# Block products for the last four up groups of an MLP, with the sums of weights made in DRAM

## The chip, the cores and the metric

The kernel runs on one core of a Trainium2 chip. Its metric is the device time of one execution in microseconds (us). The engines are TensorE (PE in the profile, with PEld for its loads of the stationary operand), VectorE (DVE), ScalarE (ACT), GpSimd (POOL) and SyncE (SP). They run at the same time, each works through its own list of instructions, and they wait for one another by semaphores. DMA transfers are issued here from SP, from ScalarE and from POOL.

## The reference

One layer of a hybrid encoder works on 512 rows of width 1024, all in float32. It has an input projection, eight heads of attention with a forget gate beside four heads of a gated recurrence, an output projection, cross attention to 256 memory rows, and an MLP. The change lies in the MLP:

```python
u = rmsnorm(h, norm_ff_g[l]) @ w1[l]
h = h + jnp.square(jax.nn.relu(u)) @ w2[l]
return rmsnorm(h, final_norm_g)
```

Here `w1` is 1024 x 4096 and `w2` is 4096 x 1024. The row factor of the inner norm is positive, so it can leave relu and square: the hidden value is r squared times relu(x w1) squared, with r one number per row.

## The kernel before

Every float32 operand of a matmul is split in two parts of a narrower format, `hi` and `lo`, and each product of a 128 x 128 stationary part with a moving part of up to 512 columns is made by three matmuls: hi hi, hi lo and lo hi. For a weight block, SP loads a raw tile, ScalarE casts it to `hi` (L175) and VectorE subtracts to get `lo` (L179). `whp` and `wlp` hold four blocks of each part, `wrp` two raw tiles.

The 4096 hidden columns are worked off in eight groups of 512. The up part of a group (`mlp_up`) makes four PSUM blocks of 128 hidden columns x 512 rows, each over eight chunks of depth 128 by `gemm_fm` (L240 to L242). ScalarE applies relu and square (L1306, L1307). The down part (`mlp_down`, L1366 to L1368) multiplies the 512 x 512 transposed hidden values with the 512 x 1024 rows of `w2`. It does so in 2 x 2 blocks with seven products in place of eight, named 1 to 7. Four of these products need sums of blocks of hidden values (`hidden_sums`, `hidden_part`), four need sums of blocks of `w2`. PSUM banks U, Y and V gather the products in the order of `PRODUCTS`, and after each product VectorE adds the bank, times plus or minus r squared (`rsq`), to the result `acc` (L1334). The down part of group g-1 follows the up part of group g. The last two groups share one down part, whose final product is cut in pieces with the final norm (`last_product`, L1393).

The sums of `w2` blocks are made in SBUF. `load_raws` loads five raw blocks per group (L1255) into a ring of eight slots. POOL issues DMAs that accumulate onto them (L1244): two add a block straight from `w2`, two add one slot to another once its former value has been split. For the up groups from the third on, four blocks of `w1` per group go through `load_unit`.

TensorE's order is the order in which the code emits it. The other engines are put in order by a planner, from priorities; the splits of the MLP have a lowered one (`ahead(PW)`). A queue of blocks, `unit_q`, keeps the next four blocks loaded and split ahead of the product in hand (`unit`).

Before the MLP, POOL computes the biases of attention (`bi`, L926, with rows of `nF` loaded by DMA), some row factors (L361, L364) and sums of squares (L1074 to L1078). Work of projections is mixed in between the steps of attention (`fill`).

Of the kernel before, what the change touches and what calls it, by code (L numbers as in the profile page):

```python
# [16 lines left out]
P = 128  # L17
# [21 lines left out]
NEG = -3.0e38  # L39


@with_exitstack
def emit(
# [189 lines left out]
    def gemm_fm(ps, wt, col, ahi, alo, n=S, order=range(KC), begun=False):  # L233
# [3 lines left out]
        for n_, k in enumerate(order):  # L237
# [5 lines left out]
            yield 3 * n / 2400  # L243

    def gemm_tm(ps, wt, ahi, alo, tb, nk=KC):
# [3 lines left out]
        for k in range(nk):  # L249
# [6 lines left out]
            yield 3 * n / 2400  # L256

    def gemm_wide(pss, ahi, alo, done):

        for half in range(2):  # L260
            whi, wlo = next_panel()
            for u in range(2):
                for tb, ps in enumerate(pss):
                    sl = slice(tb * P, (tb + 1) * P)
                    for kk in range(2):
# [5 lines left out]
                        yield 3 * S / 2400  # L271
# [127 lines left out]
    xTd = drp.tile([4, P, 2, S], F32, name="xTd")  # L399
    park = {}  # L400
# [817 lines left out]
    slots = [t[:, i, :] for t in [ap_.tile([P, 4, D], F32, tag="act", name=f"wq{j}") for j in range(2)] for i in range(4)]  # L1218
    HS = S // 2
    units, raws, unit_q = {}, {}, deque()  # L1220
    sqs, comb, hbs = {}, {}, {}

    def up_units(g):
        for j in range(2):
            spec = panel(w1, g * HG + j * WT)
            for n in range(2):

                def prep(g=g, j=j, n=n, spec=spec):
                    if (j, n) == (0, 0):
                        down_raws(g - 1)  # L1230
                    unit, splits = load_unit(f"u{g}{j}{n}", spec, slice(n * UK, (n + 1) * UK))
                    with ahead(PW):
                        for split in splits:
                            split()
                    units["u", g, j, n] = unit

                unit_q.append((("u", g, j, n), prep))

    quad = {"a1": (0, 0), "c1": (0, 0), "a2": (0, 1), "b2": (1, 1), "b1": (1, 0)}
    PRODUCTS = ("1", "2", "6", "5", "7", "3", "4")  # L1240

    def add_weights(raw, src):

        gp.dma_start(raw.rearrange("p (k n) -> p k n", k=2), src, accum_op=ALU.add)  # L1244
# [18 lines left out]
    def down_raws(g):  # L1263

        load_raws(g, RAWS)
        first_adds(g)
# [287 lines left out]
```

## Time and profile before

| | before |
|---|---|
| time, median of 3 runs | 766.79 us (766.42 to 766.93) |
| the profiled execution: time, span | 766.06 us, 764.3 us |
| TensorE busy, instructions | 755.3 us (99%), 4069 |
| VectorE busy | 502.8 us (66%) |
| ScalarE busy | 388.6 us (51%) |
| POOL busy | 170.3 us (22%) |
| granted TensorE clock | 0.999 |
| DMA | 103.01 MB, mean 135 GB/s |

The page of the profile tells for each engine the busy time, then cuts the span into 40 slices (19 us each) with the busy share in tenths. The chain of waits goes back from the last instruction to what released it, step by step, so an engine with a large share of the chain sets the time. A row of a group names the line, engine, operation, output and inputs, shapes and count, then the busy time, the mean duration in ns, and the idle time before these instructions with the engine that ended it. Records of matmuls overlap, so the rate of TensorE is read from start to start. A row of a stretch gives its bounds and, per engine, the busy time in it.

### The profile page before, as it was taken

How to read it: one execution, taken by the hardware profiler on the slowest of the kernel's cores; microseconds unless marked ns; L12 is line 12 of the kernel's file. 1: busy time of each engine (PE TensorE's matmuls, PEld its weight loads, DVE VectorE, ACT ScalarE, POOL GpSimd, SP SyncE). 2: the span in 40 equal slices, each digit the busy share in tenths (PEclk: the TensorE clock that was granted, in tenths of full speed). 3: DMA queues.
4: the chain of work that ended last, by engine and by line, in shares of the span. 5: the costliest groups of instructions: out<-in, count | busy, mean ns of one | idle time of the engine just before them, and what ended most of it. 6: DMA issues, size and time to landing. Idle time of an engine off the chain costs nothing.

```text
span 764.3 us, 10886 instructions
## 1 busy us (share of the span) xinstructions
PE 755.3 (99%) x4069; PEld 635.5 (83%) x4069; DVE 502.8 (66%) x816; ACT 388.6 (51%) x657; POOL 170.3 (22%) x248
## 2 busy tenths in 40 slices
PE   9999999999999999999999999999999999999996
PEld 6889888888889988888888888888888888888885
DVE  5647863678877656555546445939495776767596
ACT  6655554656666523344444456455454545353653
POOL 7207531322542225310000110101001010101123
PEclk9999999999999999999999999999999999999999
DMA  8652333313635432222113595575758575758602
GB/s 241 201 138 58 85 84 111 111 56 111 197 111 172 138 129 83 84 98 67 56 56 103 204 280 129 153 171 160 179 156 198 143 189 142 193 138 217 141 1 110
DMA packets 78870, 103.01 MB, mean 135 GB/s; under 512 B 4657, under 2 KB 56410, under 8 KB 78818
## 3 DMA queue, kind: packets, MB, share of 16 engines
q1 hardware_dynamic: 69266, 76.61, 32.1%
q0 software_dynamic: 8960, 24.67, 15.5%
q10 hardware_dynamic: 592, 1.05, 0.4%
q8 instruction: 32, 0.52, 0.3%
q14 instruction: 20, 0.16, 0.1%
HBM read 89.71 MB, written 4.21 MB: 123 GB/s over the span
## 4 chain that ended last, share of the span: by engine, by line
PE 95%; DVE 2%; ACT 1%; POOL 1%; issue 1%; ACTq 0%; POOLq 0%
PE u L240 8%; PE u L241 8%; PE u L242 8%; PE U L1366 4%; PE U L1367 4%; PE U L1368 4%; PE xq L240 2%; PE wo L240 2%; PE xq L241 2%; PE xq L242 2%; PE xw L241 2%; PE xw L242 2%; PE wo L242 2%; PE xw L240 2%; PE wo L241 2%; PE Y L1366 2%
## 5 line engine op out<-in xcount | busy, mean ns | idle before, releaser
L179 DVE TENSOR_TENSOR wld<-wq,whd 128x1024 fp32r<-128x1024 f32 x56 | 68.8, 1240 | 46.8 <-ACT whd L175 46.8
L240 PE MATMUL u<-x_hi,whu 128*128 128x512 f32 x192 | 74.7, 389 | 0.0
L241 PE MATMUL u<-x_lo,whu 128*128 128x512 f32 x192 | 74.7, 389 | 0.0
L242 PE MATMUL u<-x_hi,wlu 128*128 128x512 f32 x192 | 74.7, 389 | 0.0
L175 ACT ACTIVATE whd<-wq 128x1024 fp32r<-128x1024 f32 x56 | 58.3, 1052 | 29.7 <-PE u L241 18.5
L1244 POOL DMA_DIRECT2D wq<-in_w_dram x16 | 19.4, 1228 | 178.4 <-DMA wq<-in_w_dram 124.7
L175 ACT ACTIVATE whu<-wru 128x1024 fp32r<-128x1024 f32 x24 | 25.3, 1053 | 56.9 <-DMA wru<-in_w_dram 56.9
L179 DVE TENSOR_TENSOR wlu<-wru,whu 128x1024 fp32r<-128x1024 f32 x24 | 29.3, 1222 | 33.0 <-ACT whu L175 33.0
L1366 PE MATMUL U<-whd,hb 128*128 128x512 f32 x120 | 46.7, 389 | 0.0
L1367 PE MATMUL U<-wld,hb 128*128 128x512 f32 x120 | 46.7, 389 | 0.0
L1368 PE MATMUL U<-whd,hb 128*128 128x512 f32 x120 | 46.7, 389 | 0.0
L242 PEld LDWEIGHTS u<-x_hi,wlu 128*128 128x128 f32 x192 | 36.0, 188 | 7.5
L240 PEld LDWEIGHTS u<-x_hi,whu 128*128 128x128 f32 x192 | 36.0, 188 | 7.5
L241 PEld LDWEIGHTS u<-x_lo,whu 128*128 128x128 f32 x192 | 36.0, 188 | 7.4
L1244 POOL DMA_DIRECT2D wq<-wq x16 | 14.1, 880 | 125.0 <-DVE wld L179 95.6
L1334 DVE SCALAR_TENSOR_TENSOR acc<-U,rsq,acc 128x512 f32<-128x512 f32 x56 | 39.8, 744 | 0.3 <-PE U L1393 0.3
L926 POOL TENSOR_SCALAR bi<-nF,Ft 128x128 f32<-128x128 f32 (+3 forms) x32 | 23.0, 726 | 58.0 <-PE pt L958 37.0
L1306 ACT ACTIVATE sq<-u 128x512 f32<-128x512 f32 x32 | 18.7, 584 | 20.5 <-PE u L242 20.5
L1368 PEld LDWEIGHTS U<-whd,hb 128*128 128x128 f32 x120 | 22.5, 188 | 4.7
L1366 PEld LDWEIGHTS U<-whd,hb 128*128 128x128 f32 x120 | 22.5, 188 | 4.7
L1367 PEld LDWEIGHTS U<-wld,hb 128*128 128x128 f32 x120 | 22.5, 188 | 4.7
L1324 ACT ACTIVATE hb<-s 128x512 fp32r<-128x512 f32 x24 | 15.0, 629 | 20.6 <-PE U L1368 13.6
(957 smaller groups left out, 2262.1 us busy)
## 6 DMA issues: line engine op xcount, KB each, us to landing
wq<-in_w_dram SPq DMA_DIRECT2D x40, 512.0 KB, 3.4
wru<-in_w_dram SPq DMA_DIRECT2D x24, 512.0 KB, 6.4
wq<-in_w_dram POOLq DMA_DIRECT2D x16, 512.0 KB, 8.7
wq<-wq POOLq DMA_DIRECT2D x16, 512.0 KB, 4.9
xTd<-xT POOLq DMA_DIRECT2D x4, 512.0 KB, 4.1
nF<-Fd POOLq DMA_DIRECT2D x8, 256.0 KB, 3.9
hT<-xTd POOLq DMA_DIRECT2D x4, 512.0 KB, 5.3
xt<-in_x_dram SPq DMA_DIRECT2D x3, 512.0 KB
```

The source lines that it names most:

```text
L175: ac.activation(hi, raw, AF.Copy)
L179: ve.tensor_tensor(lo, raw, f(hi), ALU.subtract)
L240: te.matmul(ps, wh, hi, start=n_ == 0 and not begun, stop=False)
L241: te.matmul(ps, wh, lo, start=False, stop=False)
L242: te.matmul(ps, wl, hi, start=False, stop=k == order[-1])
L926: gp.tensor_scalar(bi[:, 0:n], fF[h][:, 0:n], -1.0, Ft[:, tb, h : h + 1], op0=ALU.mult, op1=ALU.add)
L1244: gp.dma_start(raw.rearrange("p (k n) -> p k n", k=2), src, accum_op=ALU.add)
L1306: ac.activation(u, ps, AF.Relu)
L1334: ve.scalar_tensor_tensor(a, ps, rsq[sign][:, tb : tb + 1], a, op0=ALU.mult, op1=ALU.add)
L1366: te.matmul(ps, hi, whi[:, k, :], start=begin, stop=False, skip_group_check=True)
L1367: te.matmul(ps, hi, wlo[:, k, :], start=False, stop=False, skip_group_check=True)
L1368: te.matmul(ps, lo, whi[:, k, :], start=False, stop=k == 1, skip_group_check=True)
```

## The change

The up parts of groups 4 to 7 (`SEVEN`) are also made in 2 x 2 blocks with seven products (`mlp_up7`): depth in two halves of 512, hidden columns in two halves of 256, rows in two halves of 256. Each product takes one block of four chunks, and its matmuls have 256 columns. The sums of blocks of x that four of the products need are made once, in groups 1 to 3 (`x_sums`). Banks pass their contents on by copies on ScalarE, and two blocks are completed by an add on VectorE before relu and square.

All sums of weight blocks, for `w2` in eight groups and for `w1` in four, are now made in DRAM (`sum_jobs`): each sum is a DMA that copies a block and a DMA that accumulates another onto it, eight transfers of 512 KB a set, twelve sets, all issued on POOL. `Presum` spreads their emission over the program: after 80 us of counted matmul time, one each 4.8, two sets in turn. Every product then has a block of its own to load, from the weights or from a sum, into one of five raw tiles (`raw_tile`: two from `wrp`, three from the pool `s4`). The ring of eight slots and the accumulations in SBUF go.

The order of the products becomes 1, 5, 6, 2, 7, 3, 4 in both parts. In the down part product 1 is copied from bank U to bank V by ScalarE, and product 2 adds to it, so the add of product 1 to `acc` goes. `acc` is multiplied once by the row's mean square (`e2`) so that r squared leaves the adds; the final norm takes this factor out again, with an epsilon to match (`eps3`). The hidden parts are made up to four ahead of use (`hidden_ahead`, `HB`).

```diff
+SEVEN = (4, 5, 6, 7)
+RAWS, HB = 5, 4
+PRE0, PRE = 80.0, 4.8
...
-            yield 3 * n / 2400
+            yield presum.tick(3 * n / 2400)
...
+
+    SUMS = {"5": ("00", "01"), "7": ("01", "11"), "6": ("5", "11"), "4": ("6", "10")}
+
+    def block1(g, rc):
+        r, c = int(rc[0]), int(rc[1])
+        n0 = g * HG + c * WT
+        return w1[r * S : (r + 1) * S, n0 : n0 + WT].rearrange("(k p) n -> p k n", p=P)
+
+    def block2(g, rc):
+        r, c = int(rc[0]), int(rc[1])
+        k0 = g * HG + r * 2 * P
+        return w2[k0 : k0 + 2 * P, c * S : (c + 1) * S].rearrange("(k p) n -> p k n", p=P)
+
+    wsum = {}
+
+    def sum_jobs(kind, g):
+        block, shape = (block1, [P, UK, WT]) if kind == "u" else (block2, [P, 2, S])
+        for name in SUMS:
+            wsum[kind, g, name] = drp.tile(shape, F32, name=f"ws{kind}{g}{name}")
+        for name, add in (("5", 0), ("7", 0), ("5", 1), ("7", 1), ("6", 0), ("6", 1), ("4", 0), ("4", 1)):
+            dst, (a, b) = wsum[kind, g, name], SUMS[name]
+            if add:
+                gp.dma_start(dst, block(g, b), accum_op=ALU.add)
+            else:
+                gp.dma_start(dst, wsum[kind, g, a] if a in SUMS else block(g, a))
+            yield
+
+    class Presum:
+        def __init__(self):
+            self.jobs, self.left = deque(), PRE0
+
+        def tick(self, us):
+            self.left -= us
+            while self.left <= 0.0 and self.jobs:
+                job = self.jobs[0]
+                if next(job, 0) == 0:
+                    self.jobs.popleft()
+                    continue
+                if len(self.jobs) > 1:
+                    self.jobs[0], self.jobs[1] = self.jobs[1], self.jobs[0]
+                self.left += PRE
+            return us
+
+    presum = Presum()
+    for g in range(DFF // HG):
+        presum.jobs.append(sum_jobs("d", g))
+        if g + 2 in SEVEN:
+            presum.jobs.append(sum_jobs("u", g + 2))
...
-    slots = [t[:, i, :] for t in [ap_.tile([P, 4, D], F32, tag="act", name=f"wq{j}") for j in range(2)] for i in range(4)]
...
-    units, raws, unit_q = {}, {}, deque()
+    units, unit_q = {}, deque()
     sqs, comb, hbs = {}, {}, {}
+    PRODUCTS = ("1", "5", "6", "2", "7", "3", "4")
+    QUAD = {"1": "00", "2": "10", "3": "11"}
+    raw_n = [0]
...
+    def raw_tile(name):
+        raw_n[0] += 1
+        if raw_n[0] % RAWS in (0, 2):
+            return wrp.tile([P, D], F32, tag="wr", name=f"wr{name}", padded_shape=[P, UK * UW])
+        return s4([D], f"wr{name}")
+
+    def add_unit(key, shape, src):
+
+        def prep():
+            name = "".join(map(str, key))
+            unit = new_parts(shape, name)
+            raw = raw_tile(name).rearrange("p (k n) -> p k n", k=shape[0])
+            nc.sync.dma_start(raw, src())
+            with ahead(PW):
+                split_of(unit[0], unit[1], raw)()
+            units[key] = unit
+
+        unit_q.append((key, prep))
...
+        if g in SEVEN:
+            for name in PRODUCTS:
+                add_unit(("u", g, name), [UK, WT], lambda name=name: block1(g, QUAD[name]) if name in QUAD else wsum["u", g, name])
+            return
...
-            spec = panel(w1, g * HG + j * WT)
...
-    def add_weights(raw, src):
-
-        gp.dma_start(raw.rearrange("p (k n) -> p k n", k=2), src, accum_op=ALU.add)
-
-    RAWS = ("a1", "c1", "a2", "b2", "b1")
-
-    def load_raws(g, names):
-        w = raws.setdefault(g, {})
-        for name in names:
-            r, c = quad[name]
-            n = 5 * g + RAWS.index(name)
-            w[name] = slots[n % 8] if n < 38 else k4([D], f"wq{n}")
-            src = w2[g * HG + r * 2 * P : g * HG + (r + 1) * 2 * P, c * S : (c + 1) * S].rearrange("(k p) n -> p k n", p=P)
-            nc.sync.dma_start(w[name].rearrange("p (k n) -> p k n", k=2), src)
-            w[name, "src"] = src
-
-    def first_adds(g):
-        w = raws[g]
-        add_weights(w["a2"], w["b2", "src"])
-        add_weights(w["c1"], w["a2", "src"])
...
-                for to, of in (("a1", "a2"), ("b1", "a1")):
-                    add_weights(w[to], w[of].rearrange("p (k n) -> p k n", k=2))
...
+                add_unit(("d", g, name), [2, S], lambda g=g, name=name: block2(g, QUAD[name]) if name in QUAD else wsum["d", g, name])
...
+    def mlp_up7(g):
+
+        qa, qb = (k4([2, S], f"sq{g}{j}") for j in range(2))
+        sqs[g, 0], sqs[g, 1] = qa, qb
+        h1, h2 = slice(0, HS), slice(HS, S)
+        bank = {}
+
+        for name in PRODUCTS:
+            b = {"5": "Y", "3": "Y", "2": "V"}.get(name, "U")
+            if b not in bank:
+                bank[b] = (pvt if b == "Y" else mm)(f"u{b}{g}").rearrange("p (i n) -> p i n", i=2)
+                if b == "V":
+                    pass
+            ps = bank[b]
+            whi, wlo = unit("u", g, name)
+            xh, xl = xsum[name]
+            for k in range(UK):
+                for i in range(2):
+                    ws, begin = slice(i * P, (i + 1) * P), name in "15" and k == 0 and i == 0
+                    te.matmul(ps[:, i, :], whi[:, k, ws], xh[:, k, :], start=begin, stop=False, skip_group_check=True)
+                    te.matmul(ps[:, i, :], whi[:, k, ws], xl[:, k, :], start=False, stop=False, skip_group_check=True)
+                    te.matmul(ps[:, i, :], wlo[:, k, ws], xh[:, k, :], start=False, stop=k == UK - 1, skip_group_check=True)
+                presum.tick(6 * HS / 2400)
+            if name == "1":
+                bank["V"] = mm(f"uV{g}").rearrange("p (i n) -> p i n", i=2)
+                ac.activation(bank["V"], ps, AF.Copy)
+            elif name == "5":
+                y5 = t2(f"y5{g}", F32, (2, HS))
+                ac.activation(y5, ps, AF.Copy)
+            elif name == "6":
+                ac.activation(bank["Y"], ps, AF.Copy)
+            elif name == "2":
+                square(ps, qa[:, :, h1])
+            elif name == "7":
+                ve.tensor_tensor(qb[:, :, h2], ps, y5, ALU.add)
+                square(qb[:, :, h2], qb[:, :, h2], -1.0)
+            elif name == "3":
+                ve.tensor_tensor(qb[:, :, h1], ps, y5, ALU.add)
+                square(qb[:, :, h1], qb[:, :, h1], -1.0)
+            else:
+                square(ps, qa[:, :, h2])
+            yield
...
+    def x_sums():
+
+        xs_hi, xs_lo = act_tile("xs_hi"), act_tile("xs_lo")
+        xs_hi, xs_lo = (t.rearrange("p k (h n) -> p (k h) n", h=2) for t in (xs_hi, xs_lo))
+
...
+        names = ("5", "6", "3", "7")
+        out_ = {n: tuple(t[:, i * UK : (i + 1) * UK, :] for t in (xs_hi, xs_lo)) for i, n in enumerate(names)}
+        d = s4([UK, HS], "xs_d")
+        for n, (a, b, sign) in (("5", ("4", "2a", -1)), ("6", (None, "1", 1)), ("3", (None, "2", -1)), ("7", ("1", "2a", -1))):
+            op = ALU.add if sign > 0 else ALU.subtract
+            if a is None:
+                ve.tensor_tensor(d, d, f(x_[b][0]), op)
+            else:
+                ve.tensor_tensor(d, f(x_[a][0]), f(x_[b][0]), op)
+                ve.tensor_tensor(d, d, f(x_[a][1]), ALU.add)
+            ve.tensor_tensor(d, d, f(x_[b][1]), op)
+            yield
+            hi, lo = out_[n]
+            ac.activation(hi, d, AF.Copy, scale=-1.0 if n == "6" else 1.0)
...
+                ve.tensor_tensor(lo, d, f(hi), ALU.subtract)
+            xsum[n] = (hi, lo)
+            yield
...
+    def hidden_ahead(key, n):
+
+        used = hb_order.index(key)
+        for k in hb_order[used : used + n]:
+            if k not in hbs and k[0] in comb:
+                hidden_part(*k)
...
-        ve.scalar_tensor_tensor(a, ps, rsq[sign][:, tb : tb + 1], a, op0=ALU.mult, op1=ALU.add)
...
+        a = acc[2 * rows + t][:, half * S : (half + 1) * S]
+        if sign > 0:
+            ve.tensor_tensor(a, ps, a, ALU.add)
+        else:
+            ve.scalar_tensor_tensor(a, ps, -1.0, a, op0=ALU.mult, op1=ALU.add)
...
-        "1": ("U", True, ((0, 0, 1),)),
+        "1": ("U", True, ()),
...
-        "2": ("V", True, ((0, 0, 1),)),
+        "2": ("V", False, ((0, 0, 1),)),
...
+                hidden_ahead((g, name), 1)
...
-                    banks[bank, t] = {"U": sc, "Y": tr, "V": mm}[bank](f"{bank}{g}{t}")
+                    banks[bank, t] = {"U": sc, "Y": tr}[bank](f"{bank}{g}{t}")
...
+                presum.tick(6 * S / 2400)
+                if g != gs[-1]:
+                    continue
+                if name == "1":
+                    banks["V", t] = mm(f"V{g}{t}")
+                    ac.activation(banks["V", t], ps, AF.Copy)
...
-            if not end:
-                hidden_part(gs[0] + 1, name)
-            elif n == 0:
-                hidden_part(NG - 1, PRODUCTS[1])
+            hidden_ahead((gs[-1], name), HB)
+            yield
...
-            gp.tensor_scalar(e, e, 1.0, EPS, op0=ALU.mult, op1=ALU.add)
+            gp.tensor_tensor(e, e, eps3[:, tb : tb + 1], op=ALU.add)
...
-                    for _ in range(2):
-                        unit_q.popleft()[1]()
-            else:
-                wt = tuple(list(x) for x in zip(*(unit("u", g, j, n) for n in range(2))))
-                if (g, j) == (NG - 1, 0):
-                    load_raws(g, RAWS[0:3])
...
+    xsum = {}
+
+    def mlp_up_group(g):
+        if g in SEVEN:
+            yield from mlp_up7(g)
+            return
...
-    rsqt = cp.tile([P, 2, NT], F32, name="rsq")
-    rsq = {1: rsqt[:, 0, :], -1: rsqt[:, 1, :]}
-    e2 = sm(NT, "r2e")
+    e2 = cp.tile([P, NT], F32, name="e2")
+    eps3 = cp.tile([P, NT], F32, name="eps3")
     gp.tensor_scalar(e2, ms2, 1.0, EPS, op0=ALU.mult, op1=ALU.add)
-    ve.reciprocal(rsq[1], e2)
...
+    gp.tensor_tensor(eps3, e2, e2, op=ALU.mult)
+    gp.tensor_scalar(eps3, eps3, EPS, 0.0, op0=ALU.mult, op1=ALU.add)
+    for tb in range(NT):
+        ac.activation(acc[tb], acc[tb], AF.Copy, scale=e2[:, tb : tb + 1])
...
+    sums = x_sums()
     for g in range(1, NG):
-        for up in mlp_up_group(g):
-            square(*up)
+        for n, _ in enumerate(mlp_up_group(g)):
+            hidden_ahead((g - 1, PRODUCTS[0]), min(n, HB))
+            if g < 4 and n == 1:
+                next(sums, None)
...
-            mlp_down((g - 1,))
-    load_raws(NG - 1, RAWS[3:])
-    first_adds(NG - 1)
-    hidden_part(NG - 1, PRODUCTS[0])
...
+            for n, _ in enumerate(mlp_down((g - 1,))):
+                if g < 4 and n in (2, 5):
+                    next(sums, None)
+
+    hidden_ahead((NG - 2, PRODUCTS[0]), HB)
```

More of the change, by code (lines that the diff above doesn't have):

```diff
@@ L1294, in unit, with square @@
         return got
+    def square(ps, out_, sign=1.0):
+        ac.activation(out_, ps, AF.Relu, scale=sign)
+        ac.activation(out_, out_, AF.Square)
     def mlp_up(g, j, wt):
@@ L1411, in last_product @@
                 product(ps, 1, qs, True)
-                ve.scalar_tensor_tensor(acc[3][:, qs], ps, rsq[1][:, 3:4], acc[3][:, qs], op0=ALU.mult, op1=ALU.add)
+                ve.tensor_tensor(acc[3][:, qs], ps, acc[3][:, qs], ALU.add)
                 v = squares(3, o3, qs, v, f"fv3{q}")
```

89 lines of the change are left out of this document (35 added, 54 removed).

## The prediction

> **What bounds the kernel now.** I read the page first (busy time, slices, chain), then the waits of TensorE, then stretches of the MLP stage, then groups and transfers.
>
> ```profile
> span 764.3 us, 10886 instructions
> ...
> PE 755.3 (99%) x4069; PEld 635.5 (83%) x4069; DVE 502.8 (66%) x816; ACT 388.6 (51%) x657; POOL 170.3 (22%) x248
> ...
> PE   9999999999999999999999999999999999999996
> ...
> DMA  8652333313635432222113595575758575758602
> ...
> q1 hardware_dynamic: 69266, 76.61, 32.1%
> q0 software_dynamic: 8960, 24.67, 15.5%
> ...
> PE 95%; DVE 2%; ACT 1%; POOL 1%; issue 1%; ACTq 0%; POOLq 0%
> ```
>
> TensorE is the bound from end to end: 99% busy, 95% of the chain. Its whole list of waits is two lines, and neither lies in the MLP:
>
> ```profile
> PE warm L352 <- DVE ones L356: 1.3, 1, 1.3
> PE pt L958 <- DVE bi L950: 0.7, 1, 0.7
> ```
>
> So only fewer or cheaper matmuls make it faster, and every wait that the change puts in front of TensorE is paid in full. Two stretches of the MLP, one early and one in its regular middle (columns: bounds, length, busy of PE, weight load, DVE, ACT, POOL, clock, DMA share, GB/s):
>
> ```profile
> 440.00:460.00 20.00, 20.00 (x90) 16.57 (x89) 9.56 (x13) 11.73 (x19) 2.60 (x3) 1.00 1.10 285
> ...
> 640.00:680.00 40.00, 40.00 (x179) 33.10 (x178) 28.00 (x36) 19.55 (x26) 4.18 (x4) 1.00 0.67 171
> ```
>
> TensorE is full in both, even where the DMA share is 1.10.
>
> **The change, part by part.** *Matmuls.* The price is the start-to-start time, not the duration (389 ns records overlap). The end of the chain gives it for both shapes, twelve with 512 columns and then twenty-four with 256:
>
> ```profile
> 751.77 2.72 PE U L1393 x12
> 754.49 2.88 PE Z L1393 x24
> ```
>
> 2.72/12 = 0.2267 us and 2.88/24 = 0.120 us. Half the columns cost 53% of the time, which eats part of the saving. An up group was 4 blocks x 8 chunks x 3 = 96 wide matmuls, 21.76 us. With seven block products it is 7 x 4 x 2 x 3 = 168 narrow ones, 20.16 us. Saved: 1.60 us a group, **6.4 us** in four groups. The down groups keep 84 wide matmuls, 19.04 us.
>
> The Trainium skill, "TensorE: Matmul & The Clock Gate", section "Back-to-back issue gap", gives a lone gap of N/2.4 + 2.5 ns, so 215.8 and 109.2 ns here; an estimate from it is 20.72 - 18.34 = 2.37 us a group and 9.5 us in all. The trace has 226.7 and 120, both about 11 ns above that, and more instructions pay the extra more often; the sum stays with 6.4.
>
> *VectorE and ScalarE beside TensorE.* Prices come from the groups in 520 to 720 us:
>
> ```profile
> L179 DVE TENSOR_TENSOR wld<-wq,whd 128x1024 fp32r<-128x1024 f32 x34 | 41.1, 1221 | 30.0 <-ACT whd L175 30.0
> L1334 DVE SCALAR_TENSOR_TENSOR acc<-U,rsq,acc 128x512 f32<-128x512 f32 x38 | 27.0, 744 | 0.0
> ...
> L1328 DVE TENSOR_TENSOR hb<-sq,hb 128x512 fp32r<-128x512 f32 x15 | 10.3, 686 | 1.1 <-ACT hb L1324 1.1
> ```
>
> ```profile
> L175 ACT ACTIVATE whd<-wq 128x1024 fp32r<-128x1024 f32 x34 | 35.2, 1050 | 14.4 <-PE u L241 12.7 <-DMA wq<-wq 1.7
> L175 ACT ACTIVATE whu<-wru 128x1024 fp32r<-128x1024 f32 x20 | 21.1, 1053 | 47.4 <-DMA wru<-in_w_dram 47.4
> L1307 ACT ACTIVATE sq<-sq 128x512 f32<-128x512 f32 x19 | 12.0, 633 | 0.6
> L1306 ACT ACTIVATE sq<-u 128x512 f32<-128x512 f32 x20 | 11.7, 583 | 9.7 <-PE u L242 9.7
> ```
>
> VectorE per round of one up and one down group, before: 11 splits x 1.22 + 14 adds x 0.744 + 11 halves and sums x 0.686 = 31.4 us of 40.8. After: 14 x 1.22 + 8 signed adds x 0.744 + (4 plain adds, 11 halves and sums, 2 adds in the up part) x 0.686 = 34.7 us of 39.2. ScalarE before: 11 x 1.05, 8 square steps of 0.583 or 0.633, 7 halves near 0.633, 20.9 us; after: three more splits and five bank copies at about 0.6, 27.0 us. Both stay under 39.2, so I cost them at nothing. The cover is lookahead (four blocks split ahead, four hidden halves) and, for the banks, one product between write and rewrite: 24 x 0.120 = 2.88 us in the up part, where U is copied by ScalarE after product 1 and again after 6, and read by VectorE after 7. A copy of 0.6 behind a split of 1.05 fits in 2.88. The sums of x (14 VectorE operations near 1.22, 17 us, plus four ScalarE casts) are spread over groups 1 to 3, some 6 us a round beside the 31.4, less two adds: 36 of 40.8, covered, with little left. Scaling acc once is four ScalarE passes near 1.05 us before the first add, and the rsq chain goes; nothing on TensorE. The tail keeps its instructions: nothing.
>
> *Loads on SP.* 64 become 92 transfers of 512 KB.
>
> ```profile
> wq<-in_w_dram SPq DMA_DIRECT2D x40, 512.0 KB, 3.4
> wru<-in_w_dram SPq DMA_DIRECT2D x24, 512.0 KB, 6.4
> wq<-in_w_dram POOLq DMA_DIRECT2D x16, 512.0 KB, 8.7
> wq<-wq POOLq DMA_DIRECT2D x16, 512.0 KB, 4.9
> ```
>
> A round needs 14 blocks where it needed 11 and 4 accumulations, one each 2.8 us. With five raw tiles that leaves 14 us from request to split, against landings of 3.4 to 6.4. A load of a sum waits on SP for its last accumulation, and the loads behind it wait too. By the pacing in the code (first job at 80 us of counted matmul time, one per 4.8, 96 in all) the last pair of sums is issued at 541 counted us; the MLP starts at about 326 (3 x columns/2400 summed over the matmul triples of the projections before it), a round counts 41 and one with block products 38, so the last down products start at 588 and their loads some 10 earlier; the closest pair has some 35 us to spare: nothing.
>
> *Copies and accumulations on POOL.* 32 accumulations leave, 96 transfers come, 51 of them before the MLP. Engine time of one: no transfer from DRAM to DRAM is in this trace. Two stretches with a lone accumulation, and one with a load:
>
> ```profile
> 554.00:556.00 2.00, 2.00 (x11) 1.65 (x9) 1.23 (x1) 0.34 (x2) 0.25 (x1) 1.00 0.67 131
> 556.00:558.00 2.00, 2.00 (x10) 1.69 (x9) 1.16 (x2) 1.92 (x3) 0.00 (x0) 1.00 0.71 131
> ...
> 560.00:562.00 2.00, 2.00 (x11) 1.65 (x10) 2.00 (x4) 0.93 (x3) 0.00 (x0) 1.00 1.03 385
> ```
>
> An accumulation takes 2 x (0.67 + 0.71) = 2.76 us of all 16 engines for its 0.524 MB, a load 0.524/0.385 x 1.03 = 1.40. I take 1.40 for a copy (nearest to a load: one stream) and 2.76 for an accumulation, bounds 1.40 and 2.76 for both: 48 x 4.16 = 200 us, between 134 and 265, spread over some 550 us of the run. In the MLP, loads take 0.67 x 40.8 - 4 x 2.76 = 16.3 us per 11, 1.48 each: 40% of the engines in groups 1 to 3, 53% in the last four. With paced sums (8.5 jobs per round, 2.08 each, 43%) that is 83 to 96%: tight, not over. I cost it at 0, because the row at 440 shows full engines and a full TensorE; its upper end is the first rival.
>
> POOL's own time is on the path at one place before the MLP:
>
> ```profile
> L1244 POOL DMA_DIRECT2D wq<-in_w_dram x16 | 19.4, 1228 | 178.4 <-DMA wq<-in_w_dram 124.7
> ```
>
> ```profile
> 150.11 1.03 POOL hr L364
> 151.16 0.44 POOL bi L926 x2
> ...
> 154.24 0.55 POOL m1r L364
> 154.81 1.10 DVE mt L374
> ...
> 163.87 0.30 PE pt L958
> ```
>
> The chain runs through POOL from 150 to 155 us and reaches the `pt` where TensorE waited its 0.7 us. An issue is 1.23 us; between zero and two fall into that stretch (one job per 4.8 counted us, about 6 real): 0 to 2.5 us. I take one, **+1.2**. Elsewhere `bi` waits for TensorE, not the reverse. An accumulation also waits at the head of POOL's queue for its copy to land, and `bi` and the loads of nF stand behind it; jobs of one set are two slots apart, about 12 us, over 8.7: nothing, and up to a few us if landing stretches.
>
> **Sum.** The profiled execution took 766.06 (span 764.3, the rest around it): 766.06 - 6.4 + 1.2 = 760.9. The median of the runs is 766.79, 0.7 above that execution, so 761.6. A measurement of this kernel can tell about 0.2%, 1.5 us, from no change.
>
> **Rivals.** *Loads starve (slower).* After r2e POOL has nothing but sums until the last adds, so nothing paces them:
>
> ```profile
> 441.59 0.18 POOL L1505 TENSOR_SCALAR r2e<-ms 128x4 f32<-128x4 f32 x1 [2.30 <-ACT sj L1501]
> ...
> 730.59 3.00 POOL L1458 TENSOR_TENSOR fa<-acc,gfin 128x512 f32<-128x512 f32 x2 [8.18 <-DVE acc L1334]
> ```
>
> 45 transfers, 94 us of engine time, would run in one block beside the loads. A packet of POOL's queue took 0.155 x 764.3 x 16/8960 = 211 ns, one of SP's 57 ns. If the queues take turns packet by packet, loads get 57/268 = 21%. The block then lasts 94/0.79 = 119 us, loads get 25 us of it where 40% of 119 = 48 are needed, and the nine blocks in hand (five raw, four split) are worth 9 x 1.48 = 13: TensorE advances 38/0.40 = 96 us in 119 and stands for 23. Time: 761.6 + 23 = 785. It decides from a share of about 28% for the loads downwards. Against it: each accumulation waits for a landing, so about two are in flight and the queue is often empty; 440 to 460. For it: a share of 96% without any burst.
> The Trainium skill, "DMA: Bandwidth & Descriptors", section "Queues, rings and completion order", says that each DMA engine goes round its queues packet by packet, which is this rule; the 6.4 us of the wru loads beside accumulations against 3.4 lean to it, but no wait of TensorE does.
>
> *A split holds the bank copies (slower).* ScalarE already stood 47.4 us for wru loads in that window, 2.4 per split of 20. If a split that waits so stands ahead of the copy of U, 2.4 + 1.05 + 0.6 is 1.2 over the 2.88; at the 12 blocks taken straight from w1, 14 us: 776. It decides from a wait above 1.8 us (6.4/12 over the slack). Against: five raw tiles where up loads had two.
>
> *The gain is eaten.* Five issues on the POOL chain, or some late nF, 5 to 7 us: no change, 767.
>
> *The block products run at the bare streaming rate.* 256/512 of 226.7 is 113 ns, 19.0 us a group, 11 us saved: 757. The 24-matmul row speaks against it.
>
> **How the numbers follow.** Forecast 0.50 (759 to 765, by 0 to 2.5 us on POOL and a few short waits); bare rate 0.02; eaten 0.08; starved loads 0.26; held copies 0.14. Faster 0.52, same 0.08, slower 0.40. The range goes from 758.5 to 784: below lies the bare rate, above it about half of the starved cases.
>
> **What would show it.** Right: the four up groups as trains of 168 narrow matmuls in 20.2 us, down groups unchanged, a list of TensorE's waits with little in the MLP, DMA share near 0.9 after 440 us. Wrong: waits of TensorE on ScalarE's or VectorE's splits with loads landing in over 10 us (starved), on the U copies (held), or gaps at `pt` with POOL issues ahead of `bi`.

## The result, and the profile after

The changed kernel takes 856.16 us (median of 4 runs, 854.82 to 857.96) where the kernel before takes 766.61 (765.98 to 766.93): a ratio of 1.1171, 95% interval 1.1145 to 1.1197. It is 90 us slower; the prediction said 5 us faster.

The page of the changed kernel, in the lines that answer to those shown of before:

```profile
span 853.1 us, 11657 instructions
...
PE 777.8 (91%) x4357; PEld 662.2 (78%) x4357; DVE 527.8 (62%) x834; ACT 422.8 (50%) x703; POOL 215.8 (25%) x314
...
PE   8795687757697989999999999999999999999996
...
PEclk9797798978899999999999999999999999999999
DMA  9999999999999725433311223326353646557262
...
q0 software_dynamic: 23680, 58.22, 28.5%
...
PE 64%; DMA 23%; issue 5%; POOL 4%; DVE 2%; ACT 1%; SPq 0%; ACTq 0%; POOLq 0%; DVEq 0%
```

The damage is in the first 15 slices of 21 us. TensorE is no longer full there, its granted clock falls, and the DMA engines are full from the first slice to the thirteenth. From the 16th slice on TensorE is as full as it was before. DMA now holds 23% of the chain.

Where the 96 transfers stand is told by POOL's list of that run, in order of time (start, length, line, operation, wait before it). This is the first of them and the last:

```profile
2.09 1.55 POOL L427 DMA_DIRECT2D wsd<-in_w_dram  x2
...
279.70 1.06 POOL L425 DMA_DIRECT2D wsd<-in_w_dram  x1 [0.51 <-DMA wsd<-wsd]
```

All of them are issued between 2 and 281 us. The prediction had them spread over some 550 us, from 80 counted us on. The stretches of the same run (columns as in the prediction) show what this does:

```profile
0.00:60.00 60.00, 51.34 (x217) 38.11 (x218) 27.42 (x45) 29.24 (x43) 32.65 (x66) 0.91 1.00 289
60.00:120.00 60.00, 42.80 (x335) 36.82 (x334) 25.91 (x44) 19.16 (x34) 34.29 (x41) 0.83 1.04 249
120.00:180.00 60.00, 43.54 (x267) 35.12 (x267) 27.35 (x56) 21.43 (x37) 29.67 (x43) 0.85 1.07 251
180.00:240.00 60.00, 44.91 (x230) 37.67 (x230) 22.30 (x46) 21.25 (x62) 33.95 (x51) 0.87 1.01 248
...
700.00:740.00 40.00, 40.00 (x257) 36.59 (x256) 33.07 (x42) 26.31 (x36) 0.00 (x0) 1.00 0.60 195
```

The kernel before, in the first of these stretches:

```profile
0.00:60.00 60.00, 58.61 (x313) 46.20 (x315) 35.04 (x54) 35.83 (x53) 22.32 (x49) 1.00 0.64 187
60.00:120.00 60.00, 60.00 (x497) 50.92 (x494) 42.39 (x91) 32.06 (x58) 28.21 (x38) 1.00 0.31 87
120.00:180.00 60.00, 59.31 (x385) 52.84 (x385) 36.70 (x85) 35.45 (x97) 18.25 (x39) 1.00 0.32 93
```

The DMA share (next to last column) of the changed kernel is 1.0 or more for 240 us, where the kernel before has 0.31 to 0.64, and TensorE stands for a quarter of that time (182.6 of 240 us busy). In the MLP, at 700 us, TensorE is full and POOL has nothing to do. The longest of TensorE's waits in the changed kernel (total, times, longest) all lie ahead of the MLP but for one:

```profile
PE pk L873 <- ACT A L835: 10.5, 1, 10.5
PE dg L694 <- DVE z L661: 7.2, 1, 7.2
PE pr L866 <- DVE rec L917: 6.7, 2, 6.2
...
PE gf L243 <- ACT wh1b L178: 5.1, 1, 5.1
...
PE U L1506 <- ACT hb L1426: 1.5, 1, 1.5
```

The engines that release it are late themselves. In the chain of the first 280 us (start, length, what) the long pieces are transfers. A first weight takes 13 us to land. From then on the chain runs mostly through POOL's own list: POOL stands until one sum has landed before it issues the next, and its steps that TensorE's inputs need (`mov` at first, later `bi`) come behind sums that no product takes before the MLP begins.

```profile
17.33 13.02 DMA wr1b<-in_w_in_dram
41.91 10.46 DMA wsd<-in_w_dram
...
118.72 12.81 DMA wsd<-wsd
...
239.34 15.43 DMA wsd<-in_w_dram
...
263.14 1.25 POOL bi L977 x2
```

So two causes are mixed in this chain: full DMA engines, and waits for landing on POOL's list. Runs 3, 4, 8 and 11 below are there to tell them apart.

Two points in time split every run below: the first matmul of the MLP (`u`) and the start of the last one (`Z`). The length of the MLP is the time between them, and "late" is its start against before. The times are medians, and the other columns are of the one profiled execution. Runs 3, 4, 8 and 11 are one execution each. Run 7 scatters most (770.33 to 779.0 us), and its profile is of the fastest.

| run | time, us | MLP starts | late | MLP's length |
|---|---|---|---|---|
| before | 766.6 | 429.8 | | 327.3 |
| changed | 856.16 | 523.4 | 93.6 | 323.0 |
| 1 POOL in emission order | 796.41 | 445.2 | 15.4 | 341.0 |
| 2 before, POOL in emission order | 770.16 | 430.6 | 0.8 | 329.6 |
| 3 short transfers | 771.67 | 434.3 | 4.5 | 323.1 |
| 4 plain copies, no landing waits | 820.38 | 488.9 | 59.1 | 323.1 |
| 5 paced as assumed | 769.03 | 437.2 | 7.4 | 323.5 |
| 6 paced evenly | 765.60 | 434.2 | 4.4 | 323.4 |
| 7 paced late | 772.65 | 436.6 | 6.8 | 325.3 |
| 8 down sums alone | 836.24 | 498.1 | 68.3 | 329.4 |
| 9 evenly, hidden halves early | 764.33 | 434.0 | 4.2 | 321.5 |
| 10 pacing skips the chain through POOL | 760.82 | 430.5 | 0.7 | 321.5 |
| 11 copies first | 857.82 | 526.3 | 96.5 | 323.1 |

So the changed kernel loses 93.6 us before its MLP begins and gains 4.3 in it.

### The profile page after: what moved, and what is told of

Read it like the earlier page. It is cut to its first block, busy times and chain, and to the rows that moved or that the text cites. A ratio compares the mean times of both kernels' runs of the same rounds, so it can differ in the third digit from the quotient of the medians.

```text
span 853.1 us, 11657 instructions
## 1 busy us (share of the span) xinstructions
PE 777.8 (91%) x4357; PEld 662.2 (78%) x4357; DVE 527.8 (62%) x834; ACT 422.8 (50%) x703; POOL 215.8 (25%) x314
## 4 chain that ended last, share of the span: by engine, by line
PE 64%; DMA 23%; issue 5%; POOL 4%; DVE 2%; ACT 1%; SPq 0%; ACTq 0%; POOLq 0%; DVEq 0%
DMA wsd<-in_w_dram 9%; DMA wsd<-wsd 8%; PE u L245 3%; PE u L243 3%; PE u L244 3%; PE U L1478 3%; PE U L1477 3%; PE U L1479 3%; PE uU L1352 2%; PE uU L1351 2%; PE uU L1350 2%; PE xq L243 2%; PE wo L243 2%; PE xq L244 2%; PE xw L243 2%
## 5 line engine op out<-in xcount | busy, mean ns | idle before, releaser
L182 DVE TENSOR_TENSOR wld<-wrd,whd 128x1024 fp32r<-128x1024 f32 x56 | 69.5, 1242 | 33.3 <-ACT whd L178 33.3
L178 ACT ACTIVATE whd<-wrd 128x1024 fp32r<-128x1024 f32 x56 | 59.2, 1058 | 34.2 <-PE u L244 14.2
L425 POOL DMA_DIRECT2D wsd<-in_w_dram x32 | 39.8, 1300 | 57.0 <-DMA wsd<-wsd 44.5
L999 ACT ACTIVATE bi<-bi,mx 128x128 f32<-128x128 f32 (+3 forms) x32 | 17.9, 558 | 28.3 <-DVE mx L997 28.1
L425 POOL DMA_DIRECT2D wsu<-in_w_dram x16 | 24.8, 1552 | 2.4 <-DMA wsu<-in_w_dram 1.2
L1479 PE MATMUL Y<-whd,hb 128*128 128x512 f32 x64 | 24.9, 389 | 0.0
L1477 PE MATMUL Y<-whd,hb 128*128 128x512 f32 x64 | 24.9, 389 | 0.0
L1478 PE MATMUL Y<-wld,hb 128*128 128x512 f32 x64 | 24.9, 389 | 0.0
L243 PE MATMUL u<-x_hi,whu 128*128 128x512 f32 x64 | 24.9, 389 | 0.0
L244 PE MATMUL u<-x_lo,whu 128*128 128x512 f32 x64 | 24.9, 389 | 0.0
L245 PE MATMUL u<-x_hi,wlu 128*128 128x512 f32 x64 | 24.9, 389 | 0.0
```

What stands on the lines that cost most here:

```text
L178: ac.activation(hi, raw, AF.Copy)
L182: ve.tensor_tensor(lo, raw, f(hi), ALU.subtract)
L243: te.matmul(ps, wh, hi, start=n_ == 0 and not begun, stop=False)
L244: te.matmul(ps, wh, lo, start=False, stop=False)
L245: te.matmul(ps, wl, hi, start=False, stop=k == order[-1])
L425: gp.dma_start(dst, block(g, b), accum_op=ALU.add)
```

## The experiments

The first theory after the result: TensorE's list follows the emission, but POOL's is set by the planner. A sum in DRAM waits for no buffer and no other engine, so the planner put all of them where POOL was idle first. The counter in `Presum`, which spreads the emission, spread nothing. The rival: the 96 transfers are too much wherever they stand.

### 1 and 2. POOL's list in emission order, in both kernels

```diff
-    ctx.enter_context(tc.manual_schedule(engines={mybir.EngineType.PE}))
+    ctx.enter_context(tc.manual_schedule(engines={mybir.EngineType.PE, mybir.EngineType.Pool}))
```

> The changed kernel with POOL's list kept in the order in which the code emits it, as TensorE's is; nothing else is edited, so the 96 transfers stand where the counter in the code puts them, the first after about 100 us. Theory: the 90 us were lost because the planner moved all 96 transfers to the front of POOL's list (first at 2 us, last near 280 us), and the MLP stage keeps its saving. It expects 757 to 766 us and a TensorE that is full from 420 us on, with the DMA share near 0.9 in the MLP's first half. Rival: 96 transfers of DRAM to DRAM cost TensorE their time wherever they stand. It expects over 800 us, with the waits moved into the MLP.

> The kernel before with the same single edit, POOL's list in the order of emission. It prices that edit by itself. Both theories expect 764 to 772 us: POOL had few places where the planner's order and the order of emission differ on the path. A time well above that would mean that run one holds a loss of this edit too.

The changed kernel came to 796.41 us (ratio 1.0396, 1.0381 to 1.041), between the two expectations; the kernel before to 770.16 (1.0046, 1.0033 to 1.0058), so the edit itself costs 3.5 us, 0.8 of it ahead of the MLP and most of the rest after 720 us. The first transfer now starts at 113 us, and 78 of the 93.6 us of delay are gone: the order of POOL's list carries most of the loss. But the MLP became 18 us longer than in the changed kernel. Stretches of run 1:

```profile
460.00:500.00 40.00, 37.20 (x161) 30.43 (x160) 27.31 (x28) 24.65 (x34) 9.31 (x11) 0.97 1.02 264
500.00:540.00 40.00, 32.62 (x120) 25.41 (x118) 26.88 (x35) 15.07 (x20) 11.20 (x13) 0.86 1.06 289
...
620.00:660.00 40.00, 40.00 (x261) 36.71 (x260) 32.55 (x41) 26.57 (x37) 0.00 (x0) 1.00 0.61 207
```

Its longest waits of TensorE, and the piece of its chain behind the longest:

```profile
PE u L243 <- ACT whu L178: 5.5, 1, 5.5
PE pt L1009 <- DVE bi L1001: 4.4, 1, 4.4
```

```profile
506.78 17.37 DMA wru<-in_w_dram
...
524.17 1.07 ACT whu L178
```

Once POOL has done its steps on the mean squares (at 458 us; `r2e` in the kernel before), nothing holds it, and it issues the last 46 transfers as fast as they land. The DMA share stays at 1.02 and above until 620 us, and the load on the chain takes 17 us to land. This is the prediction's first rival, in the place that it named. Its size came out smaller and longer: it had a block of 119 us and 23 us of standing, and here the block lasts 154 us and TensorE stands 10.2 us between 460 and 540 us, one wait of 2.8 us on a bank copy among them. The rest of the 18 us is matmuls at a lower clock (0.86 in the second stretch) and the cost of the edit itself, which run 2 puts at 2.3 us in the MLP. The Trainium skill, "DMA: Bandwidth & Descriptors", section "Queues, rings and completion order", has each engine take its queues in turn by packets, the rule from which the 23 were worked out; no run here shows the turns themselves.

### 3, 4, 8 and 11. What of the transfers costs the stage before the MLP

All four stay in the planner's order. Run 3 moves only 16 of 128 partitions in each transfer (64 KB) and keeps the waits for landing on POOL's list; the products take plain blocks in place of the sums. Run 4 makes 96 full-sized plain copies to places of their own, so no transfer needs another to have landed. Run 8 has no seven-product up groups, so 64 transfers are left. Run 11 issues all 48 copies before the 48 accumulations (its counter starts at 20 and gives one per 2.9). In runs 3, 4 and 11 the sums are missing or not those of the reference, so they are for timing only. In the edits below, run 3 cuts the copies in the same way, and in runs 4 and 11 a copy that would start from a sum starts from a plain block.

```diff
# 3
...
-                gp.dma_start(dst, block(g, b), accum_op=ALU.add)
+                gp.dma_start(dst[cut], block(g, b)[cut], accum_op=ALU.add)
...
# 4
-                gp.dma_start(dst, block(g, b), accum_op=ALU.add)
+                gp.dma_start(drp.tile(shape, F32, name=f"wx{kind}{g}{name}"), block(g, b))
...
# 8
-SEVEN = (4, 5, 6, 7)
+SEVEN = ()
# 11
...
+    presum.jobs.append(in_turn([job for add in (0, 1) for s in sets for job in s[add]]))
```

> The changed kernel, planner's order, with each of the 96 transfers cut to 16 of 128 partitions (64 KB for 512 KB); the waits of each accumulation for its copy stay. Products that need a sum load a plain block of weights instead, so the sums are left out of the result. Theory one, full DMA engines hold up the weight loads: 760 to 770 us, since an eighth of the bytes is left. Theory two, POOL's queue stands at the waits for landing and the gate and bias work behind it is late: landing falls from some 8 us to some 2 to 3, so a part of the loss stays, 780 to 810 us.

> The changed kernel, planner's order, all 96 transfers of 512 KB, but each a plain copy of a block into a place of its own: no transfer waits for another, and no sum is made (the result lacks the accumulations). Theory one, full DMA engines: the bytes are nearly the same, so 820 to 860 us. Theory two, waits at the head of POOL's queue: 765 to 785 us.

> The changed kernel without its seven-product up groups: all up groups by eight plain blocks, so only the 64 transfers for the down groups are left, in the planner's order. By the theory that the bytes of the transfers, started together at the beginning, cost the front, the loss before the MLP is about two thirds of 93.6 us, 62, and the MLP is that of the kernel before, 327 us to its end: some 829 us (815 to 840). If it is the order on POOL's list or the late part of the list that counts, and not the number, the loss stays near 90 and the time above 850.

> The changed kernel in the planner's order, with all 48 copies issued before the 48 accumulations, each accumulation onto the place of the copy 48 transfers ahead of it (the copies that would start from another sum start from a plain block, so some of the sums are not those of the reference). Copies and accumulations are as many and as large as in the changed kernel, but hardly one has to wait on POOL's list for another to land (116 us of such waits in the changed kernel). If the time that the transfers take of the engines is what costs the stage before the MLP (0.43 us of delay per us of it: 93.6 of 213 us in the changed kernel, 59.1 of 138 with plain copies alone), the MLP starts as late as in the changed kernel, at 515 to 535 us, and the whole takes 845 to 865 us. If the landing waits on POOL's list made the difference of 35 us between those two, it starts at 485 to 495 us: 815 to 828 us.

Measured: 771.67, 820.38, 836.24 and 857.82 us. Run 3 falls between its two theories, close to the first. Run 4 lies at the lower end of the first, and runs 8 and 11 came out as expected. Run 3 leaves 4.5 of the 93.6 us (its last rows also end some 5 us later than in the other runs; why was not found). After run 4 it looked as if the landing waits on POOL's list, 116 us in the changed kernel, made up the missing 35 us. Run 11 speaks against that: it has 36 us of such waits, not 116, and starts its MLP at 526.3 us, no earlier than the changed kernel. The delay takes another road there: the sums have 13 to 15 us from issue to landing (7 to 9 in the changed kernel), and the chain stands on loads that take up to 21. What the delay goes with is the engine time of POOL's queue. The line of that queue (packets, MB, share of 16 engines' span) in run 4 and in run 11:

```profile
q0 software_dynamic: 16128, 58.22, 20.5%
```

```profile
q0 software_dynamic: 26368, 58.22, 27.8%
```

In the kernel before the queue took 0.155 x 764.3 = 118 us, of which 32 x 2.76 = 88 were its accumulations, so about 30 us belong to other work. Take these off, and the transfers took 213 us in the changed kernel (0.285 x 853.1 - 30), 138 in run 4, 137 in run 8, 208 in run 11 and 28 in run 3. The delays of 93.6, 59.1, 68.3 and 96.5 us are 0.44, 0.43, 0.50 and 0.46 of that; for run 3, in which the DMA share is 0.77 in the first 60 us and 0.52 or less after them, it is 0.16. The bytes in run 4 and run 11 are the same, so it isn't the bytes either: an accumulation takes the engines about twice as long as a copy (below). The measure is rough: runs 4 and 8 have the same engine time, and their delays differ by 9 us. What makes up these 9 us is not shown.

Run 8 tells one more thing. Its MLP has no block products in the up groups and is 329.4 us long, 2.1 *more* than before. The changed kernel's is 323.0. So the four up groups bring 329.4 - 323.0 = 6.4 us, and another part of the change takes 2.1 back. The end of run 8's chain shows where:

```profile
821.15 0.73 ACT fo L1547
...
822.33 0.64 ACT hb L1426
823.02 1.93 PE U L1506 x6
824.94 2.88 PE Z L1506 x24
```

The hidden half of the very last product (`hb`) is made by ScalarE behind the finishing of a row block (`fo`), and TensorE stands for it 1.5 us, with six wide matmuls and the 24 of `Z` still to come.

### 5, 6 and 7. The transfers held in place

POOL's list is in emission order up to the last part of the MLP, and each transfer waits for the split that was made before it: VectorE copies one element of that split, POOL reads the copy. The numbers of the pace differ: first at 80 counted us and one per 4.8, as the prediction read the code (run 5); first at 20 and one per 5.7 (run 6); first at 203, then one per 3.0, in the MLP one per 4.3 (run 7). In the edit, the pace shown is that of run 6.

```diff
+                state["lo"] = f(lo)[:, 0, 0:1]
...
+                tok = sm(1, "tok")
+                ve.tensor_copy(tok, state["lo"])
+                gp.tensor_copy(sm(1, "tokp"), tok)
                 if next(job, 0) == 0:
...
-                self.left += PRE
+                self.left += 5.7
...
+    pool_order = tc.manual_schedule(engines={mybir.EngineType.Pool})
+    pool_order.__enter__()
...
+    pool_order.__exit__(None, None, None)
```

> The changed kernel with POOL's list in emission order up to the last part, and each transfer held until the split before it in the list has been made (VectorE copies one element of that split's low part, POOL reads the copy, then issues): the 96 transfers then stand where the prediction placed them, one per 4.8 counted us from 80 on. If the missing pacing is the whole of what went wrong, TensorE's waits of 10 us and more in the MLP are gone and its start to end there is 323 to 327 us; what stays is the share of full engines between 120 and 430 us, where the run in emission order lost 14 us, and up to 3 us that emission order alone cost in the last part: 762 to 785 us. If the bytes themselves are too many wherever they stand (96 transfers of 2.1 us of all engines beside loads that need 40 to 53% of them), it stays at 790 or above.

> As the paced run, but the first transfer at 20 counted us and one per 5.7, so that the 200 us of engine time lie evenly over the run, some 33% of the engines on top of the loads. If losses come only where the sum of loads and transfers passes the engines, this is the best of the paced runs: 760 to 778 us, with the first 120 us (DMA share 0.8 to 0.9 already from the loads there) the place where TensorE waits. If TensorE waits wherever a transfer stands beside loads, it is no better than the run paced from 80 counted us.

> As the paced run, but nothing before 203 counted us, then one per 3.0 until 326 and one per 4.3 in the MLP. The stage before 250 us is then as in the kernel before. Where losses come from full engines alone, the front loses under 3 us, and the MLP, where the share becomes 0.86 to 0.99, decides: 762 to 770 us if the loads get what they need, 775 to 790 if they starve as in the run in emission order (17 us from request to landing there).

Measured: 769.03 us (ratio 1.0035, 1.0022 to 1.0048), 765.60 (0.9987, 0.9978 to 0.9995) and 772.65 (1.0098, 1.0067 to 1.0128). All three have the same 96 transfers as the changed kernel and are 83 to 91 us faster: the theory holds, the rival of "too much wherever they stand" falls. Runs 5 and 6 lie in their ranges, and run 7 falls between its two. Run 5 in the MLP, in stretches:

```profile
540.00:580.00 40.00, 40.00 (x178) 33.11 (x178) 29.57 (x45) 21.43 (x30) 10.75 (x16) 1.00 0.91 247
580.00:620.00 40.00, 40.00 (x257) 36.59 (x256) 33.22 (x49) 26.55 (x35) 10.76 (x18) 1.00 1.00 292
```

TensorE is full beside engines at 0.91 and 1.00. Most of what run 5 loses ahead of its MLP it loses at the transposes `pt`, just before 167 us; its two longest waits ahead of the MLP after the warm-up:

```profile
PE pt L1016 <- DVE bi L1008: 4.3, 2, 3.9
...
PE pv L1032 <- DVE pts L1022: 0.9, 1, 0.9
```

What comes late there is a load: `mt`, which POOL issues right behind a sum. This piece is of the chain that leads to that wait:

```profile
152.33 7.03 DMA mt<-in_mem_dram
```

In the emission order `mt` is issued at 152 us, in the kernel before at 133. Alone that does no harm: in run 2 it is issued at 151.8 us, lands in 3.6, and `pt` doesn't wait. Beside sums it lands in 7.0 us in run 5 (3.9 us of waiting in one piece) and in 5.4 in run 6 (1.8).

Run 7 starts its output projection `wo` only 0.2 us later than before (269.4 against 269.2), so without sums beside it the front loses nothing. It then loses 3.3 us of TensorE in one stretch, where the sums come one per 3.0, and its MLP is 1.9 longer than in run 6:

```profile
300.00:340.00 40.00, 36.66 (x164) 30.52 (x163) 20.28 (x32) 10.42 (x16) 22.72 (x32) 0.91 0.88 211
```

The hold isn't free. TensorE waits 0.4 to 1.3 us in runs 6, 7 and 9 behind the copied element (`tok`) in VectorE's list.

### 9 and 10. Two losses taken out

Run 9 is run 6 with the hidden halves made six ahead in the last part. Run 10 also moves the pace: first transfer at 35 counted us, one per 3.6 up to 80, none up to 108 (118 to 162 us of the run, where TensorE's inputs come through POOL), then one per 5.5.

```diff
-            hidden_ahead((gs[-1], name), HB)
+            hidden_ahead((gs[-1], name), HB + 2 * end)
...
-                self.left += 5.7
+                self.left += 3.6 if self.sum < 80.0 else max(5.5, 108.0 - self.sum)
```

> The evenly paced kernel with one change in the last part: the hidden halves are made six ahead there, not four, so that the half for the last product is made before the rows are finished. If the 1.5 us for which TensorE stood before its last six matmuls is what separates the MLP's gain of 4.3 us from the 6.4 of the matmuls, the wait goes and the MLP takes 321 to 322 us: 763 to 764.3 us. If the wait only moves (to the row sums or to the last VectorE steps), it stays at 765 to 766.

> As the run before it, but the transfers start at 35 counted us, come one per 3.6 until 80, stop until 108 (the stage where the chain of TensorE's inputs runs through POOL, 118 to 166 us) and go on one per 5.5. If POOL's issues in that chain cost the 2 us that TensorE waited at the transposes, and the first transfers beside the first weights 0.5, the start of the MLP comes 2 to 3 us earlier (431 to 432.5 us): 760.5 to 762.5 us. If full engines at 60 to 118 us (an estimated share of 0.9) hold the loads there, it comes at 434 or later: 763 to 766.

Measured: 764.33 us (ratio 0.9973, 0.9964 to 0.9981) and 760.82 (0.9936, 0.9924 to 0.9949). Run 10 came out as expected, run 9 at the edge of it. The end of run 9's chain has its last products in one piece, and its MLP is 1.9 us shorter:

```profile
750.23 2.72 PE U L1513 x12
752.95 2.88 PE Z L1513 x24
```

Run 10 starts its MLP 3.5 us earlier than run 9. It keeps both POOL's issues and the sums' traffic out of that stage, so it doesn't tell the two apart; `mt` lands in 3.6 us again. These are all of its waits of TensorE, and lines of its page:

```profile
PE warm L356 <- DVE ones L360: 1.3, 1, 1.3
PE gi L272 <- ACT gg L652: 0.7, 1, 0.7
PE pt L1016 <- DVE bi L1008: 0.2, 1, 0.2
```

```profile
span 758.7 us, 11914 instructions
...
PE 749.8 (99%) x4357; PEld 644.4 (85%) x4357; DVE 538.1 (71%) x942; ACT 422.4 (56%) x703; POOL 258.5 (34%) x422
...
DMA  8665875355777788665547639698799898999652
```

It is faster than both kernels: by 5.7 us than the one before, under 1% but clear of the scatter, and by 95 than the changed one.

## Why the prediction was wrong, step by step

- *Matmuls, 6.4 us saved: right.* An up group by block products takes 668.45 to 688.61 us in the changed kernel, 20.16 us to the digit, and run 8 against the changed kernel gives 6.4 for four groups. The estimate of 9.5 from the Trainium skill ("TensorE: Matmul & The Clock Gate", section "Back-to-back issue gap") is 3.1 too high.

```profile
668.45 0.28 PE L1350 MATMUL uU<-x_hi,whu 128*128 128x256 f32 x1
...
688.61 0.40 PE L1477 MATMUL U<-whd,hb 128*128 128x512 f32 x1
```

- *"The tail keeps its instructions: nothing": wrong by 2.1 us.* The instructions stay, their order doesn't. A hidden half that is made four ahead comes late where products of two groups alternate. Making it six ahead gave 1.9 back (run 9).
- *VectorE and ScalarE beside TensorE, nothing: right, up to the tail.* The MLP of the changed kernel has that one wait of 1.5 us and no other, and the MLP of run 10, with the sums beside it, has none.
- *Copies and accumulations: the size was right, the place was wrong, and this is the step that failed.* 200 us of engine time were forecast and 213 came. But the prediction took "the pacing in the code (first job at 80 us of counted matmul time, one per 4.8...)" for the pacing of the run, counted "51 of them before the MLP" and spread them "over some 550 us". The counter orders the emission, and only TensorE's list follows the emission. POOL's is made by the planner, and a transfer from DRAM to DRAM has nothing to wait for. In place of 51 there were 96 before the MLP, all in the first 281 us. There the engines were full. An estimate of the damage: at their share of 1.03 over the first 287 us they did 296 us of work, 213 of it for the sums, so 83 were left for all else. By its stretches (0.64 x 60 + 0.31 x 60 + 0.32 x 60 + 0.46 x 15) the kernel before had used that much by 195 us. That would put TensorE 92 us behind; it was 93.6. Where the same transfers are paced, they take no less engine time (0.339 x 758.7 - 30 = 227 us in run 10), and the MLP starts 0.7 us late.
- *"that is 83 to 96%: tight, not over. I cost it at 0": right where they are paced.* Run 5 has shares of 0.90 to 1.00 from 460 to 700 us, and TensorE stands for 0.1 us of that time.
- *POOL on the path at 150 to 155 us, +1.2 (0 to 2.5): the place was right, the reason and the size were not.* The term was one issue of 1.23 us on POOL. What costs there is the load `mt` that lands late beside a sum. With the assumed pacing TensorE waits 4.3 us at `pt` (run 5), with the even one 2.0 (run 6), and with the stage left out 0.2 (run 10). In the changed kernel this term is drowned in the rest.
- *The rivals.* Starved loads were seen as a mechanism and put in the wrong stage. The reason given ("nothing paces them", since POOL is free after `r2e`) holds from the first microsecond on: nothing ever paced them. The prediction asked what would hold POOL after 441 us and not what would hold it before. Held bank copies are in none of the waits of the changed kernel's MLP; run 1 has one of 2.8 us, run 7 one of 0.3. The list of what would prove it wrong did name loads landing in over 10 us, but as the sign of that rival in the MLP.

Run 5 is the kernel that the prediction had in mind: 769.03 us, not 761.6. In spans, 764.3 - 6.4 + 1.2 = 759.1 was forecast and 767.4 came, 8.3 more. The MLP starts 7.4 us late in place of 1.2. TensorE's waits there are 4.9 us longer than before (4.3 at `pt`, 0.9 at `pv` and 0.4 at `gf`, less the 0.7 at `pt` that the kernel before has too). After the stop at `pt` the granted clock is 0.63 and 0.52 for two stretches of 2 us, which is another (0.37 + 0.48) x 2 = 1.7. The last 0.8 is not assigned. The MLP is 2.6 us longer than forecast (2.1 of them as in run 8). What follows the last `Z` is 0.5 shorter.

## What to carry to other kernels

A DMA that waits for nothing has no place in time: before costing it as "spread", ask for its engine which list it stands in, who makes that list, and which earlier instruction would hold it back. If there is none, price it at the first moment at which its engine is idle, beside the loads that run there. Where early work must come late, give it something to wait for (here one element of a split), and keep it out of the stage where the chain runs through its own engine.

## What the hardware showed that was not expected

*Half the clock after a short stop.* In the changed kernel TensorE stands from 131.1 to 134.4 us for POOL. Stretches from there (the eighth column, counting the bounds as one, is the granted clock):

```profile
131.00:134.00 3.00, 0.08 (x1) 0.00 (x0) 0.00 (x0) 0.00 (x0) 2.18 (x4) 1.00 0.75 201
...
135.00:141.00 6.00, 4.88 (x34) 3.90 (x31) 3.59 (x7) 3.94 (x7) 2.67 (x5) 0.50 1.17 257
141.00:142.00 1.00, 1.00 (x6) 0.79 (x5) 1.00 (x5) 1.00 (x3) 0.00 (x0) 0.91 1.23 461
```

A stop of 3.3 us is followed by some 6.6 us at about half the clock. The Trainium skill, "TensorE: Matmul & The Clock Gate", section "Part 1: The HAM clock gate", tells of this: an idle window of about 3.4 us halves the clock, and a busy one of that length restores it. The trace agrees in kind, with a stop of 3.3 us; the slow time lasted twice as long as the stop. It is dear: the same 4357 matmuls keep TensorE busy for 777.8 us in the changed kernel (mean granted clock 0.955) and 749.8 in run 10 (0.998). Of the 94.4 us between the two spans 28 are thus slower matmuls and 66 TensorE standing, and a wait was priced in the prediction without the slow matmuls behind it.

*An accumulation in DRAM costs two copies.* 96 plain copies of 512 KB took 138 us of all 16 engines, 1.44 each. In run 11 48 of them and 48 accumulations took 208, so an accumulation took (208 - 48 x 1.44)/48 = 2.9 us. The same working gives 3.0 in the changed kernel (213) and 2.8 in run 8 (137, 32 of each). The prediction's 1.40 and 2.76, taken from loads and from accumulations into SBUF, were good for DRAM too.
